# Two pairs of feed-forward chunks by seven half-depth products, the others with activations stationary, in a two-layer trunk on one core

## The chip, the cores and the metric

The kernel runs on one core of a Trainium2 chip. TensorE (PE in the views, its weight loads PEld) does the matmuls, VectorE (DVE) and ScalarE (ACT) the elementwise work, GpSimd (POOL) a few small operations, and SyncE (SP) issues the DMAs. The metric is the device time of one execution in microseconds, as the median over runs.

## What is computed

Two layers over x of 256 rows by 1024 columns, in float32. Each layer is a half-step SwiGLU feed-forward block, a mixer (a causal convolution module in layer 0, stick-breaking attention in layer 1) and a second feed-forward block; a root-mean-square norm stands ahead of each and at the end.

```python
D_MODEL, D_FF, SEQ, DEPTH = 1024, 2816, 256, 2
def swiglu_ffn(h, w_in, w_out):
    gate, up = jnp.split(h @ w_in, 2, axis=-1)
    return (jax.nn.silu(gate) * up) @ w_out
for i in range(DEPTH):
    g = norm_g[i]
    x = x + 0.5 * swiglu_ffn(rms_norm(x, g[0]), ffn_w_in[i, 0], ffn_w_out[i, 0])
    h = rms_norm(x, g[1])
    x = x + mixer(h)                 # conformer_conv in layer 0, attention in layer 1
    x = x + 0.5 * swiglu_ffn(rms_norm(x, g[2]), ffn_w_in[i, 1], ffn_w_out[i, 1])
return rms_norm(x, final_g)
```

There are thus four feed-forward blocks, here called FFN(0,0), FFN(0,1), FFN(1,0) and FFN(1,1), and they hold most of the matmuls.

## The kernel before

**Precision.** A float32 product is made of three matmuls: each operand is split into a rounded part `hi` and a rest `lo`, and `mm3` (L177) adds hi·hi, hi·lo and lo·hi. `split` (L147) makes the two parts: a ScalarE copy for hi, then a VectorE subtraction for lo. Weights arrive by DMA in float32 in a `raw` tile (pool `rawp`, 3 buffers) and are split into a `hi` and a `lo` tile (pool `ring`, 6 buffers of each).

**One feed-forward block.** The 256 rows are two tiles t = 0, 1 of 128. D_FF is cut into 11 chunks of 256 columns; a chunk j has 256 gate columns and 256 up columns, so 512 columns of `w_in`, 1024 deep, in two weight units of half the depth. `xT` holds the transposed, split input of both tiles, with the gain of the norm in it but not the row's factor `rstd`; that is applied behind the product. The chunks' outputs are multiplied with their rows of `w_out` by `V` (L309), 12 matmuls of 512 columns for each t, and add up in four PSUM banks `psv`. The V of a chunk stands one chunk later in the code, so that TensorE has work while VectorE and ScalarE make the gate.

A chunk has one of two forms. With activations stationary (`u_mm`, L227) each tile takes 24 matmuls of 512 columns into a PSUM tile `psu`; the gate (L267) makes a 128x256 tile, which TensorE turns by two transposes (`A`, L277) into V's stationary operand `ah`, `al`. With weights stationary (`C`, L287) the result comes out turned: `u_cm` (L235) runs four times in a chunk, for each half of the columns once for gate and once for up, with 8 matmuls of 512 columns (`psc`, L242 and L245) and 8 of 256 (L243). ScalarE and VectorE then add two halves (L247, L248), multiply by the row factors `rrow` (L294; on GpSimd in L298), and gate. Before the change chunk 0 (in FFN(0,0) chunks 0 and 1) has the first form and all others the second.

**Order.** Inside the feed-forward blocks a scheduler orders each engine's queue from the code and the tiles' dependencies. Each engine then works its queue in order: an instruction that waits holds up what stands behind it. In the convolution layer and at the very start of the kernel the order is written out by hand. The hand-written convolution casts the next block's first weight units in its course: `cast(nxt[0])` (L625) stands behind the taps of channel groups 6 and 7 for row tile 0 and ahead of those for row tile 1; the tap tables `wb` (L478) take buffers of the `ring` under the tags hi and lo too. `norm(0)` (L629) stands behind that cast on VectorE, and the turn of its result (`turn`, L556) is what TensorE does next after the last taps.

Of the kernel before, what the change touches and what calls it, by code (L numbers as in the profile page):

```python
# [8 lines left out]
F32 = mybir.dt.float32  # L9
F32R = mybir.dt.float32r  # L10
# [22 lines left out]
def trunk_kernel(  # L33
# [6 lines left out]
):  # L40
    nc = tc.nc
    first_pool = ctx.enter_context(tc.tile_pool(name="first_pool", bufs=1))
    ring = ctx.enter_context(tc.tile_pool(name="ring", bufs=6))
    operands = ctx.enter_context(tc.tile_pool(name="operands", bufs=1))
    rawp = ctx.enter_context(tc.tile_pool(name="rawp", bufs=3))
    acts = ctx.enter_context(tc.tile_pool(name="acts", bufs=1))
    const = ctx.enter_context(tc.tile_pool(name="const", bufs=1))
    wk = ctx.enter_context(tc.tile_pool(name="wk", bufs=2))
# [167 lines left out]
    def boundary(t, gi):  # L216

        for q in range(2):
            split_x(t, q, gain(turn_x(t, q), gi, q))
        return *operand(t), rms_stats(t)  # L220

    def u_step(ps, t, k, units):
        h, l = operand(t)
# [38 lines left out]

    def ffn(i, f, gi, hTs, next_gi, first=None, start=None, hook=None, final=False):
        w_in, w_out = ffn_w_in[i, f], ffn_w_out[i, f]
        act, aT = {}, {}

        def gate(t, j, ps):  # L267
            rstd = hTs[t][2]
# [18 lines left out]
        def C(j, units, rrow):  # L287

            hs, ls = [], []
            for q in range(2):  # L290
                for c in range(2):
                    u = u_cm([w[:, :, c, q * P : (q + 1) * P] for w in unit] for unit in units)
                    if c == 0:
                        nc.vector.tensor_tensor(u, u, rrow, op=ALU.mult)  # L294
# [3 lines left out]
                        nc.gpsimd.tensor_tensor(a, a, rrow, op=ALU.mult)  # L298
                    else:
                        nc.vector.tensor_tensor(a, a, u, op=ALU.mult)  # L300
                ah = operands.tile([P, T, P], F32R, tag="H", bufs=4, name=nm("ah"))
                al = operands.tile([P, T, P], F32R, tag="L", bufs=4, name=nm("al"))
                split(ah, al, a)
                hs.append(ah)
                ls.append(al)
            for t in range(T):
                aT[t, j] = [h[:, t, :] for h in hs], [l[:, t, :] for l in ls]

        def V(t, j, unit, qs=(0, 1)):  # L309
            ah, al = aT[t, j]  # L310
# [59 lines left out]
            for t in range(T)  # L370
        ]
        outs, vus = [None, None], []
        for j in range(NJ):
            if j == 0 and first:
                units = first
            elif not start or j >= lead:
                units = load_pairs(w_in, 256 * j, DFF + 256 * j, 256, pieces=2 if j else 4)
            if j == 0 or j >= lead:
                vus += [load_rows(w_out, 2 * c) for c in range(len(vus), j + 1)]
            if j == lead:  # L380
                rrow = row_rstd(hTs)
            if j < lead:
                if not start:
                    for t in range(T):
                        gate(t, j, u_mm(t, units))
                for t in range(T):
                    A(t, j)
            else:
                C(j, units, rrow)
            if j == NJ - 1:  # L390
                V(0, j - 1, vus[j - 1])
                V(1, j - 1, vus[j - 1], (0,))
                V(0, j, vus[j])
                finish = end_final if final else end
                outs[0] = finish(0)
                V(1, j - 1, vus[j - 1], (1,))
                V(1, j, vus[j])
                outs[1] = finish(1)
            elif j:
                for t in range(T):  # L400
                    V(t, j - 1, vus[j - 1])
            if j == 5 and hook:
                hook()
        return outs


# [397 lines left out]
    def start(gate):  # L804
# [31 lines left out]
        with tc.manual_schedule(engines={E.PE, E.SP, E.Activation, E.DVE}):  # L836
# [10 lines left out]
            xgs = [gain(pts[q], 0, q) for q in range(2)]  # L847
            for q in range(2):
                split_x(0, q, xgs[q])
            keep_busy(8)  # L850
            pts = [turn_x(1, q) for q in range(2)]
            cast(0, 0)
# [12 lines left out]
            mm(0, (1, 1), (1, 2), (0, 3))  # L865
            cast(0, 5)
            rstds.append(rms_stats(1))
            hTs.extend((*operand(t), rstds[t]) for t in range(T))
            mm(0, (1, 3), (0, 4))
            cast(0, 6)  # L870
            mm(0, (1, 4), (0, 5))
# [50 lines left out]
```

## Time and profile before

| | |
|---|---|
| median of 3 runs (lowest, highest) | 992.16 us (991.88 to 992.81) |
| the profiled execution: its time, its span | 992.41 us, 990.6 us |
| mean granted TensorE clock | 0.997 |
| busy share PE, PEld, DVE, ACT, POOL | 99%, 82%, 73%, 52%, 13% |
| HBM read | 171.10 MB |

The profiled execution's time is 1.8 us more than its span, which runs from the first to the last instruction. The share of an engine is its busy time over that span. Matmuls overlap in the records, so that of PE says only that something was always in flight.

### The profile page before, as it was taken

What the parts mean: (1) busy time and instruction counts of PE and PEld (TensorE: products, weight loads), DVE (VectorE), ACT (ScalarE), POOL (GpSimd) and SP (SyncE); (2) the same over time, 40 slices, a digit from 0 to 9 for tenths busy, and PEclk for the clock granted to TensorE, in tenths of its full rate; (3) what the DMA queues carried; (4) which work ended last, traced back from release to release, by engine and by line L of the source; (5) the groups of instructions that cost most, each with busy time, mean ns of one, the idle gap of its engine ahead of it and who ended that gap; (6) DMA issues with size and microseconds to landing.
All of it is one profiled execution on the core that took longest, in us unless ns stands there. A gap on an engine that the chain in (4) does not pass through costs nothing.

```text
span 990.6 us, 14730 instructions
## 1 busy us (share of the span) xinstructions
PE 977.4 (99%) x5658; PEld 813.6 (82%) x5658; DVE 722.3 (73%) x1127; ACT 514.0 (52%) x873; POOL 132.8 (13%) x165
## 2 busy tenths in 40 slices
PE   8999999999999999999999999999999999999996
PEld 7888888886788888888888888888777688888885
DVE  5886767659869776767876767676867887767654
ACT  6664545355437555455554545454644455554532
POOL 3011111100001111111211111112100011111111
PEclk9999999999999999999999999999999999999998
DMA  7976564447736564646456565654633344646411
GB/s 256 314 242 219 193 228 148 152 125 224 226 96 223 170 229 151 227 155 216 155 192 203 171 211 165 218 152 154 205 126 130 120 153 157 230 151 223 160 43 42
DMA packets 142630, 177.17 MB, mean 179 GB/s; under 512 B 6393, under 2 KB 125792, under 8 KB 142560
## 3 DMA queue, kind: packets, MB, share of 16 engines
q1 hardware_dynamic: 142208, 175.69, 54.5%
q8 instruction: 44, 0.72, 0.3%
q10 hardware_dynamic: 352, 0.55, 0.1%
q14 instruction: 26, 0.21, 0.1%
HBM read 171.10 MB, written 1.05 MB: 174 GB/s over the span
## 4 chain that ended last, share of the span: by engine, by line
PE 92%; DVE 3%; issue 2%; ACT 1%; DMA 1%; POOL 0%; SPq 0%; POOLq 0%; ACTq 0%; DVEq 0%
PE psc L242 28%; PE psc L243 16%; PE psv L178 8%; PE psv L180 8%; PE psv L179 8%; PE psc L245 4%; PE psu L178 3%; PE psu L179 3%; PE psu L180 3%; PE pc L506 3%; DVE lo L149 2%; PE ptr L200 1%; PE pz L700 1%; DMA raw<-in_ffn_w_in_dram 1%; ACT hi L148 1%
## 5 line engine op out<-in xcount | busy, mean ns | idle before, releaser
L149 DVE TENSOR_TENSOR lo<-raw,hi 128x1024 fp32r<-128x1024 f32 (+1 forms) x358 | 398.9, 1137 | 79.4 <-ACT hi L148 79.0
L242 PE MATMUL psc<-xT,hi 128*128 128x512 f32 x1204 | 433.4, 399 | 0.1
L148 ACT CAST hi<-raw 128x1024 fp32r<-128x1024 f32 (+1 forms) x360 | 327.5, 952 | 89.4 <-PE psc L242 34.1
L243 PE MATMUL psc<-xT,lo 128*128 128x256 f32 x1376 | 358.8, 281 | 0.0
L243 PEld LDWEIGHTS psc<-xT,lo 128*128 128x128 f32 x1376 | 260.0, 189 | 15.6 <-issue 0.4
L242 PEld LDWEIGHTS psc<-xT,hi 128*128 128x128 f32 x1204 | 226.6, 188 | 49.3 <-DVE u L248 0.4
L298 POOL TENSOR_TENSOR s<-s,rrow 128x256 f32<-128x256 f32 x78 | 90.7, 1163 | 580.1 <-DVE s L297 580.1
L178 PE MATMUL psv<-hi,ah 128*128 128x512 f32 x354 | 138.2, 390 | 0.3
L179 PE MATMUL psv<-lo,ah 128*128 128x512 f32 x354 | 137.6, 389 | 0.0
L180 PE MATMUL psv<-hi,al 128*128 128x512 f32 x354 | 137.1, 389 | 0.0
L247 ACT COPY u<-psc 128x256 f32<-128x256 f32 x172 | 63.5, 369 | 130.0 <-PE psc L245 129.9
L248 DVE TENSOR_TENSOR u<-psc,u 128x256 f32<-128x256 f32 x172 | 72.5, 421 | 78.4 <-ACT u L247 77.7
L148 ACT CAST ah<-s 128x256 fp32r<-128x256 f32 x78 | 31.7, 407 | 92.2 <-DVE s L300 92.0
L179 PEld LDWEIGHTS psv<-lo,ah 128*128 128x128 f32 x354 | 66.6, 188 | 13.8
L180 PEld LDWEIGHTS psv<-hi,al 128*128 128x128 f32 x354 | 66.4, 188 | 13.8
L178 PEld LDWEIGHTS psv<-hi,ah 128*128 128x128 f32 x354 | 66.5, 188 | 13.3 <-ACT ah L148 1.4
L178 PE MATMUL psu<-hi,xT 128*128 128x512 f32 x176 | 70.2, 399 | 0.2 <-ACT hi L148 0.2
L179 PE MATMUL psu<-lo,xT 128*128 128x512 f32 x176 | 69.3, 394 | 0.8 <-DVE lo L149 0.6
L180 PE MATMUL psu<-hi,xT 128*128 128x512 f32 x176 | 68.9, 391 | 0.0
L245 PE MATMUL psc<-xT,hi 128*128 128x512 f32 x172 | 68.4, 398 | 0.0
L296 ACT ACTIVATE s<-u 128x256 f32<-128x256 f32 x78 | 32.4, 415 | 47.7 <-DVE u L294 47.7
L149 DVE TENSOR_TENSOR al<-s,ah 128x256 fp32r<-128x256 f32 x78 | 33.0, 422 | 21.1 <-ACT ah L148 20.9
(134 smaller groups left out, 800.6 us busy)
## 6 DMA issues: line engine op xcount, KB each, us to landing
raw<-in_ffn_w_in_dram SPq DMA_DIRECT2D x168, 512.0 KB, 4.6
raw<-in_ffn_w_out_dram SPq DMA_DIRECT2D x44, 1024.0 KB, 4.8
raw<-in_conv_w_pw_dram SPq DMA_DIRECT2D x16, 512.0 KB, 4.6
raw<-in_attn_w_qkv_dram SPq DMA_DIRECT2D x16, 512.0 KB, 5.1
raw<-in_ffn_w_in_dram SPq DMA_DIRECT2D x16, 256.0 KB, 5.0
raw<-in_conv_w_pw_dram SPq DMA_DIRECT2D x4, 1024.0 KB, 4.9
raw<-in_attn_w_qkv_dram SPq DMA_DIRECT2D x4, 1024.0 KB, 5.0
raw<-in_attn_w_o_dram SPq DMA_DIRECT2D x4, 1024.0 KB, 4.7
```

The costliest lines, as they stand in the source:

```text
L148: copy(hi, src)
L149: (eng or nc.vector).tensor_tensor(lo, src, hi.bitcast(F32), op=ALU.subtract)
L178: nc.tensor.matmul(ps, lh, rh, start=start, stop=False)
L179: nc.tensor.matmul(ps, lh, rl, start=False, stop=False)
L180: nc.tensor.matmul(ps, ll, rh, start=False, stop=stop)
L242: nc.tensor.matmul(ps, h, xT[:, :, k, :, :], start=k == 0, stop=False)
L243: nc.tensor.matmul(ps[:, :, 0, :], l, xT[:, :, k, 0, :], start=False, stop=False)
L245: nc.tensor.matmul(ps, h, xT[:, :, k, :, :], start=False, stop=True)
L247: nc.scalar.copy(u, ps[:, :, 1, :])
L248: nc.vector.tensor_tensor(u, ps[:, :, 0, :], u, op=ALU.add)
L296: nc.scalar.activation(a, u, AF.Sigmoid)
L298: nc.gpsimd.tensor_tensor(a, a, rrow, op=ALU.mult)
```

## The change

Each block now follows a plan, `UUnUSUSUUUU`. U is a chunk with activations stationary. S is a pair of chunks by `strassen`. The letter n stands for `normalize`, which from then on puts the row factor into `xT` itself, so that the gate (`gate_normal`) has no factor any more. It also makes four sums and differences of quarters of the turned input (s1 to s4), each split again. The form C isn't used any more.

`strassen` takes the two row tiles and the two halves of the depth as a 2 by 2 matrix, the two halves of the depth and the two chunks as another, and multiplies them by seven products of half depth (12 matmuls of 512 columns each) where eight stood (Winograd's form). The weight differences are made in place in the raw tiles by `less`, the seven weight operands are split in 14 pieces of 128x1024, the sums of products are made by `plus` (seven of 128x512) with two copies out of PSUM by ScalarE (`keep`). `later` puts the V of the chunk ahead between the products. The pool `ring` goes from 6 buffers of each tag to 5, `rawp` from 3 to 5.

```diff
-    ring = ctx.enter_context(tc.tile_pool(name="ring", bufs=6))
+    ring = ctx.enter_context(tc.tile_pool(name="ring", bufs=5))
-    rawp = ctx.enter_context(tc.tile_pool(name="rawp", bufs=3))
+    rawp = ctx.enter_context(tc.tile_pool(name="rawp", bufs=5))
...
+        def gate_normal(t, j, src):
+            s = wk.tile([P, 256], F32, tag="A", bufs=13, name=nm("s"))
+            nc.scalar.activation(s, src[:, 0:256], AF.Sigmoid)
+            nc.vector.tensor_tensor(s, src[:, 0:256], s, op=ALU.mult)
+            nc.vector.tensor_tensor(s, src[:, 256:512], s, op=ALU.mult)
+            act[t, j] = s
...
+        def normalize():
+            x11, x12, x21, x22 = (xg for t in range(T) for xg in hTs[t][3])
+            for n, xg in enumerate((x11, x12, x21, x22)):
+                t, q = divmod(n, 2)
+                nc.vector.tensor_tensor(
+                    xg, xg, rrow[:, t, :].unsqueeze(1).broadcast_to([P, 4, P]), op=ALU.mult
+                )
+                split_x(t, q, xg)
+            normal.append(True)
+            def operand_of(dst, a, b, op):
+                nc.vector.tensor_tensor(dst, a, b, op=op)
+                hl = wk.tile([P, 2, 4, P], F32R, tag="sk", bufs=4, name=nm("sx"))
+                split(hl[:, 0], hl[:, 1], dst)
+                return hl[:, 0], hl[:, 1]
+            s1 = operand_of(x22, x21, x22, ALU.add)
+            s3 = operand_of(x21, x11, x21, ALU.subtract)
+            s2 = operand_of(x11, x22, x11, ALU.subtract)
+            s4 = operand_of(x12, x12, x11, ALU.subtract)
...
+        def strassen(ja, jb, later):
...
+            def cast(src):
+                hi, lo = (ring.tile([P, 4, 2, 256], F32R, tag=tag, name=nm(tag)) for tag in ("hi", "lo"))
+                for ks in pieces:
+                    split(hi[:, ks], lo[:, ks], src[:, ks])
+                return hi, lo
+            def less(dst, a, b):
+                for ks in pieces:
+                    nc.vector.tensor_tensor(dst[:, ks], a[:, ks], b[:, ks], op=ALU.subtract)
+            def product(ps, x, w):
+                for k in range(4):
+                    mm3(ps, x[0][:, k, :], x[1][:, k, :], w[0][:, k], w[1][:, k], k == 0, k == 3)
...
+            w = cast(b11)
+            product(px, old(0, 0), w)
+            less(b11, b12, b11)
+            w = cast(b11)
+            p1 = keep(px)
+            product(py, s1, w)
+            less(b11, b22, b11)
+            w = cast(b11)
+            p5 = keep(py)
+            product(px, s2, w)
+            w = cast(b21)
+            u2 = plus(px, p1)
+            product(py, old(0, 1), w)
+            later(0)
+            less(b12, b22, b12)
+            w = cast(b12)
+            gate_normal(0, ja, plus(py, p1, p1))
+            product(px, s3, w)
+            less(b21, b21, b11)
+            w = cast(b21)
+            u3 = plus(px, u2)
+            plus(u2, p5, u2)
+            product(py, old(1, 1), w)
+            gate_normal(1, jb, plus(u3, p5, p5))
+            w = cast(b22)
+            gate_normal(1, ja, plus(py, u3, u3))
+            product(px, s4, w)
+            gate_normal(0, jb, plus(px, u2, u2))
+            A(0, ja)
+            A(1, jb)
+            later(1)
+            A(1, ja)
+            A(0, jb)
...
+        plan = list("UUnUSUSUUUU" if start else "UUnUSUSUUUU")
...
+            if kind == "S":
+                before = waiting
+                def later(t):
+                    for c, tt in before:
+                        if tt == t:
+                            V(t, c, vus[c])
+                strassen(j, j + 1, later)
+                load_vus(j + 1)
+                waiting = [(j, 0), (j + 1, 1), (j, 1), (j + 1, 0)]
+                j += 2
...
+                if kind == "U":
+                    if j >= lead or not start:
+                        for t in range(T):
+                            gate(t, j, u_mm(t, units))
+                    for t in range(T):
+                        A(t, j)
...
+                else:
+                    finish_waiting()
+                    waiting = [(j, t) for t in range(T)]
```

The change moves instructions at three places that matter below. In the rows a name's trailing numbers are buffer numbers, and the brackets say on which engine or DMA queue an instruction waits.

**VectorE in the convolution layer.** `lo` is the rest of the next block's first weight unit (`cast(nxt[0])`), `pl` the turned tap results of row tile 0, x the residual, z the norm's result. Before:

```order
L622 TENSOR_TENSOR x_86<-x_86,b_2139 128x1024
L149 TENSOR_TENSOR lo_2731<-raw_2460,hi_2730 128x512 [waits DMAHW2_49,DMAHW1_49,Activation_49]
L149 TENSOR_TENSOR lo_2731<-raw_2460,hi_2730 128x512 [waits Activation_49] x3
L534 BN_STATS st_2613<-pl_2774 128x6 [waits PE_49]
L540 BN_AGGR mv_2814<-st_2613 128x2 [waits DVE_49]
L547 SCALAR_TENSOR_TENSOR z_2820<-pl_2614,mv_2814,fg 128x512 [waits DVE_49]
```

and now:

```order
L766 TENSOR_TENSOR x_86<-x_86,b_1965 128x1024
L149 TENSOR_TENSOR lo_2557<-raw_2286,hi_2556 128x512 [waits DMAHW1_49,DVE_49,DMAHW2_49,PE_49,Activation_49]
L149 TENSOR_TENSOR lo_2557<-raw_2286,hi_2556 128x512 [waits Activation_49] x3
L678 BN_STATS st_2439<-pl_2600 128x6
L684 BN_AGGR mv_2640<-st_2439 128x2 [waits DVE_49]
L691 SCALAR_TENSOR_TENSOR z_2646<-pl_2440,mv_2640,fg 128x512 [waits DVE_49]
```

The order is the same; with one buffer less the lo tile takes over the buffer of the tap table of channel groups 6 and 7, and so waits for TensorE, for the last matmul of `taps(7, 1)`; the statistics behind it no longer need a wait of their own. The hi tile takes over that of groups 4 and 5, and waits for `taps(5, 1)`.

**ScalarE where FFN(0,1) begins.** The first `hi` row is the second unit of its first chunk (`cast(nxt[1])`), the later ones weight units of the block; xg is the next block's input, quarter by quarter. Before:

```order
L148 CAST hi_3011<-raw_2557 128x512 [waits DMAHW4_49,DMAHW3_49]
L148 CAST hi_3011<-raw_2557 128x512 x3
L148 CAST xT<-xg_3052 128x4x128 [waits DVE_49,Activation_49]
L148 CAST hi_3129<-raw_3128 128x1024 [waits DMAHW5_49,PE_49]
L148 CAST hi_3129<-raw_3128 128x1024
L148 CAST xT<-xg_3061 128x4x128 [waits DVE_49,Activation_49]
```

and now:

```order
L148 CAST hi_2837<-raw_2383 128x512 [waits DMAHW4_49,DMAHW3_49,PE_49]
L148 CAST hi_2837<-raw_2383 128x512 x3
L148 CAST hi_2955<-raw_2954 128x1024 [waits DMAHW5_49,PE_49]
L148 CAST hi_2955<-raw_2954 128x1024
L148 CAST hi_3048<-raw_3047 128x1024 [waits DMAHW7_49,DMAHW6_49,PE_49]
L148 CAST xT<-xg_2878 128x4x128 [waits DVE_49,Activation_49]
L148 CAST hi_3048<-raw_3047 128x1024
L148 CAST hi_3057<-raw_3056 128x1024 [waits DMAHW1_49,DMAHW0_49,PE_49]
L148 CAST hi_3057<-raw_3056 128x1024
L148 CAST xT<-xg_2887 128x4x128 [waits DVE_49,Activation_49]
```

The first cast now waits for TensorE: its buffer comes free with the second k of the convolution's last output product, `out_mm(1, 1)`. Two more weight units have moved ahead of the quarters of the input.

**VectorE where a later block passes from its second chunk to the first S.** The rows are of FFN(0,1); the two other later blocks have the same order. Here `p`, `a` are the gate of the second chunk, `lo_3212` the second unit of the third chunk, `lo_3221` its `w_out` rows, `lo_3338` the split of b11. Before, a block's chunk of the form C looks like this:

```order
L149 TENSOR_TENSOR lo_7983<-raw_7981,hi_7982 128x1024 [waits Activation_49]
L248 TENSOR_TENSOR u_7931<-psc_7914,u_7931 128x256 [waits Activation_49]
L149 TENSOR_TENSOR lo_8115<-raw_8113,hi_8114 128x1024 [waits DMAHW7_49,DMAHW0_49,Activation_49]
L300 TENSOR_TENSOR s_7910<-s_7910,u_7931 128x256 [waits DVE_49,Pool_49]
L149 TENSOR_TENSOR lo_8115<-raw_8113,hi_8114 128x1024 [waits Activation_49]
L149 TENSOR_TENSOR al_7936<-s_7910,ah_7935 128x256 [waits Activation_49]
```

and now there stands, from the moment at which the second chunk's last matmul is done:

```order
L149 TENSOR_TENSOR xT<-xg_2930,xT 128x4x128 [waits PE_49,Activation_49]
L149 TENSOR_TENSOR lo_3212<-raw_3210,hi_3211 128x1024 [waits DMAHW7_49,DMAHW6_49,Activation_49]
L149 TENSOR_TENSOR lo_3212<-raw_3210,hi_3211 128x1024 [waits Activation_49]
L284 SCALAR_TENSOR_TENSOR p_3131<-psu_3104,rstd_441_2948,s_3129 128x256 [waits DMAHW3_49,Activation_49]
...
L335 TENSOR_TENSOR xg_2939<-xg_2930,xg_2939 128x512 [waits DVE_49]
L149 TENSOR_TENSOR lo_3221<-raw_3219,hi_3220 128x1024
L149 TENSOR_TENSOR sx_3186<-xg_2939,sx_3186 128x512 [waits Activation_49]
...
L273 TENSOR_TENSOR s_3252<-psu_3227,s_3252 128x256 [waits Activation_49]
L366 TENSOR_TENSOR raw_3323<-raw_3326,raw_3323 128x1024 [waits DMAHW4_49,DMAHW3_49]
L274 TENSOR_TENSOR s_3252<-psu_3227,s_3252 128x256 [waits DVE_49]
L366 TENSOR_TENSOR raw_3323<-raw_3326,raw_3323 128x1024
```

The new split of tile 1's input waits until the second chunk, which still reads the old one, has ended on TensorE; the four sums, the weights of the third chunk and the first weight differences all stand behind it in VectorE's queue.

## Rows read from the trace of the kernel before

**Rows 1.** the page: busy us (share of the span), instructions of each engine

```profile
PE 977.4 (99%) x5658; PEld 813.6 (82%) x5658; DVE 722.3 (73%) x1127; ACT 514.0 (52%) x873; POOL 132.8 (13%) x165
```

**Rows 2.** timeline of PE, chunk 1 of FFN(0,0): start, us, engine, line, operation

```profile
12.11 0.40 PE L179 MATMUL psu<-lo,xT 128*128 128x512 f32 x1
...
31.42 0.39 PE L180 MATMUL psu<-hi,xT 128*128 128x512 f32 x1
```

**Rows 3.** timeline of PE, two of the four u_cm of a chunk C

```profile
568.03 0.39 PE L242 MATMUL psc<-xT,hi 128*128 128x512 f32 x1
...
570.84 0.40 PE L242 MATMUL psc<-xT,hi 128*128 128x512 f32 x1
```

**Rows 4.** timeline of PE, from one turn of a gated tile to past the next

```profile
36.13 0.38 PE L281 MATMUL ptr<-ident,a 128*128 128x128 f32 x2
...
37.27 0.40 PE L179 MATMUL psv<-lo,ah 128*128 128x512 f32 x1
```

**Rows 5.** timeline of DVE, 128x1024 operations

```profile
246.94 4.63 DVE L149 TENSOR_TENSOR lo<-raw,hi 128x1024 fp32r<-128x1024 f32 x4
251.49 0.35 DVE L465 SCALAR_TENSOR_TENSOR up<-ptr,vec,sg 128x128 f32<-128x128 f32 x1
...
263.57 2.36 DVE L622 TENSOR_TENSOR x<-x,b 128x1024 f32<-128x1024 f32 x2
```

**Rows 6.** timeline of DVE, operations of 128x512 and of 128x256

```profile
302.56 0.68 DVE L206 TENSOR_TENSOR xg<-ptr,gvec 128x512 f32<-128x512 f32 x1
303.16 1.22 DVE L149 TENSOR_TENSOR lo<-raw,hi 128x1024 fp32r<-128x1024 f32 x1
...
316.12 0.42 DVE L149 TENSOR_TENSOR al<-ptr,ah 128x256 fp32r<-128x256 f32 x1
316.45 0.48 DVE L274 SCALAR_TENSOR_TENSOR a<-psu,rstd,p 128x256 f32<-128x256 f32 x1
...
560.37 0.42 DVE L248 TENSOR_TENSOR u<-psc,u 128x256 f32<-128x256 f32 x1 [0.91 <-ACT u L247]
560.83 0.43 DVE L294 TENSOR_TENSOR u<-u,rrow 128x256 f32<-128x256 f32 x1
```

**Rows 7.** timeline of PE, the last taps and the turn

```profile
271.77 2.15 PE L506 MATMUL pc<-sk,wb 128*32 128x128 f32 x67
274.56 1.94 PE L506 MATMUL pc<-sk,wb 128*32 128x128 f32 x61 [0.64 <-issue]
276.43 1.09 PE L560 MATMUL ptr<-ident,m 128*128 128x128 f32 x8
```

**Rows 8.** timeline of DVE, the cast of nxt[0] and norm(0)

```profile
267.90 2.50 DVE L149 TENSOR_TENSOR lo<-raw,hi 128x512 fp32r<-128x512 f32 x4 [1.98 <-ACT hi L148]
270.32 0.69 DVE L534 BATCH_NORM_STATS2 st<-pl 128x6 f32<-128x512 f32 x1
...
274.05 1.42 DVE L554 TENSOR_TENSOR m<-z,m 128x512 f32<-128x512 f32 x2
```

**Rows 9.** timeline of ACT, the casts of nxt[0] and nxt[1]

```profile
267.26 2.17 ACT L148 CAST hi<-raw 128x512 fp32r<-128x512 f32 x4
...
287.26 2.19 ACT L148 CAST hi<-raw 128x512 fp32r<-128x512 f32 x4
```

**Rows 10.** timeline of PE, out_mm(1, 1) and the start of FFN(0,1)

```profile
297.44 0.39 PE L180 MATMUL psv<-hi,xT 128*128 128x512 f32 x1
...
302.11 0.48 PE L178 MATMUL psu<-hi,xT 128*128 128x512 f32 x1
```

**Rows 11.** windows at the end: start:end, length, busy us (count) by engine, then granted clock

```profile
984.00:985.00 1.00, 0.00 (x0) 0.00 (x0) 0.56 (x3) 0.40 (x2) 0.00 (x0) 1.00 0.25 88
...
986.00:987.00 1.00, 0.00 (x0) 0.00 (x0) 0.75 (x1) 0.72 (x1) 0.00 (x0) 0.50 0.00 0
```

**Rows 12.** timeline of PE, turns of the input at the very start

```profile
4.09 1.86 PE L200 MATMUL ptr<-ident,x 128*128 128x128 f32 x8
...
6.66 1.04 PE L200 MATMUL ptr<-ident,x 128*128 128x128 f32 x8
```

More of the change, by code (lines that the diff above doesn't have):

```diff
@@ L216, in boundary @@
     def boundary(t, gi):
+        xgs = []
         for q in range(2):
-            split_x(t, q, gain(turn_x(t, q), gi, q))
-        return *operand(t), rms_stats(t)
+            xgs.append(gain(turn_x(t, q), gi, q))
+            split_x(t, q, xgs[q])
+        return *operand(t), rms_stats(t), xgs
     def u_step(ps, t, k, units):
@@ L264, in ffn @@
         w_in, w_out = ffn_w_in[i, f], ffn_w_out[i, f]
-        act, aT = {}, {}
+        act, aT, normal, sums = {}, {}, [], []
+        def gate_normal(t, j, src):
[4 more added lines that the diff above has]
+            act[t, j] = s
         def gate(t, j, ps):
+            if normal:
+                return gate_normal(t, j, ps)
             rstd = hTs[t][2]
@@ L297, in C @@
                         nc.vector.tensor_tensor(a, a, u, op=ALU.mult)
-                        nc.gpsimd.tensor_tensor(a, a, rrow, op=ALU.mult)
+                        if not normal:
+                            nc.gpsimd.tensor_tensor(a, a, rrow, op=ALU.mult)
                     else:
@@ new lines, in strassen, with old, plus, keep @@
+        def strassen(ja, jb, later):
+            wv = w_in.rearrange("(k p) n -> p k n", p=P)
+            raw = {}
+            for h, j in ((0, ja), (0, jb), (1, jb), (1, ja)):
+                raw[h, j] = rawp.tile([P, 4, 2, 256], F32, tag="raw", name=nm("raw"))
+                for c in range(2):
+                    c0 = c * DFF + 256 * j
+                    nc.sync.dma_start(raw[h, j][:, :, c, :], wv[:, 4 * h : 4 * h + 4, c0 : c0 + 256])
+            b11, b12, b21, b22 = raw[0, ja], raw[0, jb], raw[1, ja], raw[1, jb]
+            pieces = [slice(0, 2), slice(2, 4)]
+            def cast(src):
[9 more added lines that the diff above has]
+                    mm3(ps, x[0][:, k, :], x[1][:, k, :], w[0][:, k], w[1][:, k], k == 0, k == 3)
+            def old(t, q):
+                h, l = operand(t)
+                return h[:, 4 * q : 4 * q + 4, :], l[:, 4 * q : 4 * q + 4, :]
+            def plus(a, b, dst=None):
+                if dst is None:
+                    dst = wk.tile([P, 512], F32, tag="B", bufs=4, name=nm("sum"))
+                nc.vector.tensor_tensor(dst, a, b, op=ALU.add)
+                return dst
+            def keep(src):
+                dst = wk.tile([P, 512], F32, tag="B", bufs=4, name=nm("kept"))
+                nc.scalar.copy(dst, src)
+                return dst
+            s1, s2, s3, s4 = sums
+            px, py = (ps_u.tile([P, 512], F32, tag="u", name=nm("psp")) for _ in range(2))
+            w = cast(b11)
[31 more added lines that the diff above has]
+            A(0, jb)
@@ L372, in ffn @@
         outs, vus = [None, None], []
[L373 to L380, printed above, removed]
-                rrow = row_rstd(hTs)
-            if j < lead:
-                if not start:
-                    for t in range(T):
[L385 to L402, printed above, removed]
@@ L403, in ffn @@
                 hook()
+                hook = None
         return outs
@@ L846, in start @@
             pts = [turn_x(0, q) for q in range(2)]
-            xgs = [gain(pts[q], 0, q) for q in range(2)]
+            first_xgs = [gain(pts[q], 0, q) for q in range(2)]
             for q in range(2):
-                split_x(0, q, xgs[q])
+                split_x(0, q, first_xgs[q])
             keep_busy(8)
@@ L867, in start @@
             rstds.append(rms_stats(1))
-            hTs.extend((*operand(t), rstds[t]) for t in range(T))
+            hTs.extend((*operand(t), rstds[t], (first_xgs, xgs)[t]) for t in range(T))
             mm(0, (1, 3), (0, 4))
```

36 lines of the change are left out of this document (35 added, 1 removed).

## The prediction

> **What bounds the kernel now.** I read the page's busy shares first. TensorE is busy for 99% of the span, its weight loads for 82%, VectorE for 73% [rows 1]; with nearly no idle time left on TensorE, an edit gains what it takes off TensorE's queue, and loses each new wait of TensorE. Then I read TensorE's timeline for prices. A 512-column matmul takes 0.227 us in a row of its kind: 86 of them lie from the first to the last row of [rows 2], 19.31 us over 85 steps. One `u_cm` takes 2.81 us [rows 3], so a chunk C takes 4 x 2.81 = 11.25. Two transposes put between matmuls cost 0.23: in [rows 4], 1.14 us hold three matmuls of V (0.68) and two such pairs. VectorE next. Operations of 128x1024, two float32 inputs each, follow one another at 1.138 us (4.55 for four; the residual's addition, also float32, has the same length) [rows 5]. One of 128x512 takes 0.60; one of 128x256 takes 0.33 where it is independent of the one before, 0.46 where it needs its result [rows 6]. I take 0.61 and 0.40, with 0.33 and 0.46 as bounds.
>
> **What TensorE saves.** A chunk U takes 48 matmuls and two pairs of transposes, 48 x 0.227 + 0.46 = 11.34, 0.09 more than C (0.06 with 2.82 for `u_cm`, which other chunks show; I take 0.06). A pair S takes 7 x 12 = 84 matmuls and four pairs of transposes, 19.04 + 0.92 = 19.96, against 4 x 2 x 2.82 = 22.56 for two chunks C: -2.6. V doesn't change. FFN(0,0) trades five C for U and two pairs for S: -5.2 + 0.3 = -4.9. A later block trades six and two pairs: -4.84, three blocks -14.5. In all -19.4.
>
> **What VectorE gets.** A pair S adds eight `less` and seven `plus`, a block's `normalize` four products, four sums and eight splits. A chunk C had twelve operations of 128x256 beside its weights (5.1 us), a U has six (2.5). Summed by these prices VectorE goes from 722 us to some 840, 84% of the span and above the 82% of the weight loads. Judging engines by occupancy, the Trainium skill ("Perfetto Trace Analysis", Identifying the Most-Contended Engine) names the one with the highest as the one to improve, and counts for TensorE the weight loads, not the matmuls. By that rule VectorE becomes the bound on average; I count stage by stage, since its load isn't even.
>
> *First S of a later block.* The split of tile 1's normalised input waits until chunk 1's last matmul; from there VectorE's queue is full until the first lo piece of the next U. It holds 31 operations of 128x1024 (14 lo and 8 `less` of S, 2 for the second weight unit of chunk 2, 2 for its V, 4 for the V of the pair, the first of the next U), 15 of 128x512 behind that first split (the other split of tile 1, four sums, four splits of them, seven `plus`; 16 with the first), and 22 of 128x256. With 1.4 us until the first split ends (estimate: ScalarE's copy, as long as VectorE's 0.6, and the waits between engines), that is 1.4 + 31 x 1.138 + 16 x 0.61 + 22 x 0.40 = 55.2 (one 128x512 is counted too much, 0.6, for waits inside). TensorE has, up to the second matmul of that U, 222 matmuls (the V of chunk 0, chunk 2, the V of chunk 1, 84 of S, the V of chunk 2, and 30 more of V and U that the order puts ahead) and eight pairs of transposes: 222 x 0.227 + 1.8 = 52.2. TensorE waits 3.1 us (with 0.33 or 0.46: 1.6 to 4.4).
>
> *Second S of a later block.* From the end of the U between: VectorE 0.65 until the gate begins, 25 x 1.138 + 7 x 0.61 + 16 x 0.40 = 39.8; TensorE has 168 matmuls, since the V of two chunks lies in it, and six pairs: 39.5. Wait 0.3 (0 to 1.5). Together 3.4 for a block, **10.2** for three.
>
> *FFN(0,0).* There TensorE has less beside S. First S: 142 matmuls and six pairs, 33.6, against 0.6 + 24 x 1.138 + 4.3 + 6.4 = 38.6: 5.0. Second S: 158 matmuls and the small transposes of the convolution's constants, 37.7, against 39.8 and about 1 for copying those: 3.1, to which I add 0.5 because one copy waits for its transpose. The normalised input is some 1.2 late for chunk 2, since VectorE splits weights nearly without a gap there, and five raw buffers give back about 0.5. Sum 5.0 + 3.6 + 0.7 = 9.3 (6 to 12), net of the saving **+4.4**.
>
> **What the smaller ring does to the convolution.** The cast of the next block's first unit ran on ScalarE from 267.26 and on VectorE from 267.90 to 270.32; the statistics and `norm(0)` follow in VectorE's queue and end at 275.47 (274.05 + 1.42), and TensorE turned the result at 276.43, when its taps ended, waiting for nothing [rows 7 to 9]. Now the hi part waits for `taps(5, 1)` and the lo part for `taps(7, 1)`, which is TensorE's last work ahead of the turn. The hi casts, from about 271.3, hold two evictions of taps behind them on ScalarE, and since the taps of groups 6 and 7 need their PSUM buffers, `taps(7, 1)` ends near 277.7, not 276.5. Then come four lo pieces (2.4 us, [rows 8]), and from the first statistics to the end of the gating 5.15 us (270.32 to 275.47): 277.7 + 2.5 + 5.2 = 285.4. TensorE turns at 285.4 in place of 276.43, **+9.0** (8 to 10), of which it stands idle for 7.6. Nothing covers that: all TensorE work behind the turn needs its result.
>
> **TensorE's clock after that wait.** At the end of the kernel, with TensorE's last matmul started at 982.7, and nothing after it, the granted clock was 1.00 in the window from 984 and 0.50 in that from 986 [rows 11], 1.2 in place of 2.4 GHz. A wait of 7.6 us is longer than that idle stretch up to 986. What the return costs is shown by no row directly; the nearest is the very start, where eight transposes took 1.86 us from 4.09 and 1.04 from 6.66 [rows 12]; work at half pace lasted from 1.7 to about 5.8, so some 2 us were lost. I take **+2** (0 to 4). The Trainium skill ("TensorE: Matmul & The Clock Gate", Terms) puts such a loss at half of the time at the low clock; by it the 4.1 us at the start cost 2.05, the same.
>
> **Start of FFN(0,1).** Before, nxt[1] was cast from 287.26 [rows 9], long ahead. Now it waits for the second k of `out_mm(1, 1)`, whose last matmul began at 297.44 [rows 10]: 2.2 us from 297.7, then two pieces and one more of about 0.96 each (estimate from a half piece at 0.55 in [rows 9]), then xT: near 303.4 in place of 297, and the second quarter near 306.9. `psu` began at 302.11 [rows 10], and half its work, twelve matmuls, needs the second quarter (304.8 at the old pace). **+2.5** (0 to 4).
>
> **Nothing** for attention (order alone changes near its end; 1.5 either way) and for GpSimd, which loses L298. DMA reads the same bytes.
>
> **Sum.** Against the profiled execution's 992.41 (990.6 of span and 1.8 around it; 0.25 above the median): -14.5 + 10.2 + 4.4 + 9.0 + 2.0 + 2.5 = +13.6, so 1006.0, as a median **1005.8**.
>
> **Rivals.**
> *Each long wait costs the clock too.* The first S of each block and the second of FFN(0,0) make TensorE wait 3 to 5 us. If these waits lie in one piece, as the idle time at the end did, each costs up to 2 us again: 5 x 2 = 10, about 1016. For it: VectorE's queue feeds one product after another, and the wait falls at the end, at the next U. Against: the missing pieces come in one by one, with a product of 2.7 us between.
> *VectorE keeps ahead, and it is faster.* This takes the other side. If VectorE enters each S with its first differences and splits done, because it used gaps that my count leaves out, then the waits of 10.2 and 8.6 are gone, and the sum is -5.2: 987. It decides where that lead is more than 3 us in a later block and 5 in the first. Against it stands the order: the split of tile 1 waits for TensorE, and what could run ahead is queued behind it.
> *Half of that lead* gives 996, and with no cost for the clock and the start some 992, no difference. That the change does nothing can't be; the convolution's wait is certain from the order.
>
> **Chances.** Forecast, 998 to 1013: 0.58. Clock at each S, 1013 to 1024: 0.20. Above: 0.04. Between 994.1 and 998: 0.03. A measurement of this kernel can tell about 0.2% (2 us) from no change: within that 0.05, faster 0.10. So slower 0.85. The range must leave out no more than 0.2: from 992, with no cost for clock and start and half the waits, to 1020, the clock at most S stages. The forecast's own is 998 to 1013.
>
> **What would show it.** TensorE idle for 7 to 8 us in the convolution, ahead of the `ptr` of L556's turn, released by VectorE's m; the granted clock under 1 behind it. No chunk C; the U from 11.3 us. VectorE near 100% in each S and some 840 us in all; TensorE's waits there released by lo. `psu` of FFN(0,1) waiting for xT. I am wrong if VectorE shows gaps in S (prices or lead wrong), if the wait in S is far above 4 us a block, or if the turn comes before 283 on the new time line.

## The result: 0.9% slower, 1000.92 against 992.02 us

| | before | changed |
|---|---|---|
| median (lowest, highest) | 992.02 us (991.50 to 992.81), 4 runs | 1000.92 us (999.22 to 1002.69), 4 runs |
| ratio, 95% interval | | 1.0089 (1.0066 to 1.0113) |
| profiled execution: time, span | 992.41, 990.6 | 1002.69, 1000.6 |
| mean granted clock | 0.997 | 0.993 |

The change costs 8.9 us. The forecast was 1005.8, in a range from 992 to 1020, and slower with a chance of 0.85. The profiled execution lies 1.8 us above the median; the stages below are its own, +10.3.

First the page, busy shares and the engines of the chain that ended last:

```profile
PE 970.1 (97%) x5094; PEld 778.0 (78%) x5094; DVE 811.4 (81%) x1125; ACT 524.8 (52%) x813; POOL 41.8 (4%) x87
...
PE 84%; DVE 7%; ACT 4%; DMA 3%; issue 2%; SPq 1%; POOLq 0%; ACTq 0%; DVEq 0%
```

Against [rows 1], TensorE has 564 matmuls less and 97% in place of 99%: it now waits. VectorE has risen to 81%, past the weight loads' 78%. Then the waits of TensorE: what waited for what, us in total, times, the longest:

```profile
PE ptr L704 <- DVE m L698: 7.0, 1, 7.0
PE psv L178 <- ACT ah L148: 3.6, 4, 1.8
PE pc L650 <- ACT acc L656: 2.0, 1, 2.0
PE psv L179 <- DVE lo L149: 1.9, 4, 0.9
...
PE psu L180 <- DVE xT L149: 0.9, 1, 0.9
PE psp L179 <- DVE lo L149: 0.9, 1, 0.9
```

One wait of 7.0 us stands out, that of the turn in the convolution for VectorE's m. The waits for `ah` and, in `psv` and `psp`, for lo are all of FFN(0,0). To see what each stage gained or lost I take, in TensorE's timeline of both kernels, the start of the last turn of the input that ends each stage (the convolution ends at the first such turn, since in the changed kernel the second lies inside the next block):

| stage | before, us | changed, us | difference |
|---|---|---|---|
| to the end of FFN(0,0) | 197.83 | 205.80 | +8.0 |
| convolution | 97.59 | 107.98 | +10.4 |
| FFN(0,1) with its start | 194.60 | 193.43 | -1.2 |
| FFN(1,0) | 186.52 | 182.78 | -3.7 |
| attention | 123.14 | 122.69 | -0.5 |
| FFN(1,1) to the last matmul | 183.01 | 179.94 | -3.1 |

**The convolution.** TensorE's timeline of the changed kernel, the last taps and the two turns, as in [rows 7]:

```profile
282.38 3.70 PE L650 MATMUL pc<-sk,wb 128*32 128x128 f32 x128 [1.97 <-ACT acc L656]
293.10 1.97 PE L704 MATMUL ptr<-ident,m 128*128 128x128 f32 x8 [7.02 <-DVE m L698]
...
304.03 1.03 PE L704 MATMUL ptr<-ident,m 128*128 128x128 f32 x8
```

and VectorE's, the rows that answer to [rows 8]:

```profile
286.20 2.50 DVE L149 TENSOR_TENSOR lo<-raw,hi 128x512 fp32r<-128x512 f32 x4 [12.32 <-issue]
288.62 0.69 DVE L678 BATCH_NORM_STATS2 st<-pl 128x6 f32<-128x512 f32 x1
...
292.35 1.41 DVE L698 TENSOR_TENSOR m<-z,m 128x512 f32<-128x512 f32 x2
```

The four lo pieces began at 286.20, 0.12 us after the last taps (from 282.38, 3.70 us long), and the statistics, which no longer wait for anything of their own, began at 288.62 behind them. The view names no releaser for the 12.32 us that VectorE stood idle ahead of the pieces ("issue"); that it was TensorE follows from the time and from the wait in the program's order, and the experiments below test it. The turn started 7.02 us after TensorE had run out of work. Less what was already late, 8.0, it is 293.10 - 276.43 - 8.0 = 8.7 us later. The taps themselves show 1.97 us of waiting for ScalarE's eviction, which stood behind the hi casts.

The granted clock behind it (windows: start:end, length, busy us (count) of PE, PEld, DVE, ACT and POOL, then the clock, DMA share and rate in GB/s):

```profile
289.00:291.00 2.00, 0.00 (x0) 0.00 (x0) 1.93 (x5) 0.00 (x0) 0.74 (x2) 0.90 0.56 125
291.00:293.00 2.00, 0.00 (x0) 0.00 (x0) 1.97 (x3) 1.22 (x3) 0.00 (x0) 0.50 0.97 397
...
295.00:297.00 2.00, 2.00 (x9) 1.71 (x7) 1.84 (x3) 0.59 (x1) 0.00 (x0) 0.50 0.00 0
297.00:299.00 2.00, 2.00 (x9) 1.66 (x8) 1.93 (x5) 0.00 (x0) 0.74 (x2) 0.89 0.00 0
```

It fell to 0.50 in the idle time and rose in the window from 297. From the first turn to the second it was 304.03 - 293.10 = 10.9 us; before, [rows 7] to its second turn (285.67), 9.2. That is 1.7 for the clock.

**Start of FFN(0,1).** TensorE's first `psu` matmuls there, as in [rows 10]:

```profile
321.83 0.50 PE L178 MATMUL psu<-hi,xT 128*128 128x512 f32 x1 [0.48 <-ACT xT L148]
...
323.50 0.50 PE L180 MATMUL psu<-hi,xT 128*128 128x512 f32 x1 [0.94 <-DVE xT L149]
```

`psu` begins 8.05 us after the first turn of the input (313.78); before it was 6.69 (302.11 less 295.42). With the 0.94 behind it 2.3 us are lost here.

### The profile page after: what moved, and what is told of

Read it like the earlier page. It is cut to its first block, busy times and chain, and to the rows that moved or that the text cites. A ratio compares the mean times of both kernels' runs of the same rounds, so it can differ in the third digit from the quotient of the medians.

```text
span 1000.6 us, 13490 instructions
## 1 busy us (share of the span) xinstructions
PE 970.1 (97%) x5094; PEld 778.0 (78%) x5094; DVE 811.4 (81%) x1125; ACT 524.8 (52%) x813; POOL 41.8 (4%) x87
## 4 chain that ended last, share of the span: by engine, by line
PE 84%; DVE 7%; ACT 4%; DMA 3%; issue 2%; SPq 1%; POOLq 0%; ACTq 0%; DVEq 0%
PE psu L180 12%; PE psu L179 12%; PE psu L178 12%; PE psv L179 8%; PE psv L180 8%; PE psv L178 8%; PE psp L179 4%; PE psp L178 4%; PE psp L180 4%; DVE lo L149 3%; PE psc L244 3%; ACT hi L148 3%; PE pc L650 2%; PE ptr L293 2%; PE psc L245 2%
## 5 line engine op out<-in xcount | busy, mean ns | idle before, releaser
L149 DVE TENSOR_TENSOR lo<-raw,hi 128x1024 fp32r<-128x1024 f32 (+1 forms) x406 | 439.8, 1122 | 74.5 <-ACT hi L148 59.2
L148 ACT CAST hi<-raw 128x1024 fp32r<-128x1024 f32 (+1 forms) x408 | 372.8, 965 | 152.5 <-PE psu L180 52.2
L178 PE MATMUL psu<-hi,xT 128*128 128x512 f32 x544 | 213.3, 394 | 0.9 <-ACT xT L148 0.5
L180 PE MATMUL psu<-hi,xT 128*128 128x512 f32 x544 | 212.4, 390 | 0.9 <-DVE xT L149 0.9
L179 PE MATMUL psu<-lo,xT 128*128 128x512 f32 x544 | 212.4, 390 | 0.8 <-DVE lo L149 0.5
L178 PEld LDWEIGHTS psu<-hi,xT 128*128 128x128 f32 x544 | 102.2, 188 | 23.5 <-issue 1.2
L180 PEld LDWEIGHTS psu<-hi,xT 128*128 128x128 f32 x544 | 102.1, 188 | 22.7 <-DVE xT L149 1.7
L179 PEld LDWEIGHTS psu<-lo,xT 128*128 128x128 f32 x544 | 102.2, 188 | 22.6 <-DVE lo L149 1.1
L366 DVE TENSOR_TENSOR raw<-raw,raw 128x1024 f32<-128x1024 f32 x64 | 76.3, 1215 | 0.0
L179 PE MATMUL psp<-lo,sx 128*128 128x512 f32 x128 | 50.7, 396 | 0.1
L178 PE MATMUL psp<-hi,sx 128*128 128x512 f32 x128 | 50.3, 393 | 0.0
L180 PE MATMUL psp<-hi,sx 128*128 128x512 f32 x128 | 50.3, 393 | 0.0
L149 DVE TENSOR_TENSOR al<-ptr,ah 128x256 fp32r<-128x256 f32 x88 | 36.2, 416 | 6.4 <-ACT ah L148 6.3
```

The lines of the kernel that those rows point to most:

```text
L148: copy(hi, src)
L149: (eng or nc.vector).tensor_tensor(lo, src, hi.bitcast(F32), op=ALU.subtract)
L178: nc.tensor.matmul(ps, lh, rh, start=start, stop=False)
L179: nc.tensor.matmul(ps, lh, rl, start=False, stop=False)
L180: nc.tensor.matmul(ps, ll, rh, start=False, stop=stop)
L366: nc.vector.tensor_tensor(dst[:, ks], a[:, ks], b[:, ks], op=ALU.subtract)
```

## The experiments

Ratios are to the kernel before, run on the same chip.

**Only the pools changed.** The kernel before, with

```diff
-    ring = ctx.enter_context(tc.tile_pool(name="ring", bufs=6))
+    ring = ctx.enter_context(tc.tile_pool(name="ring", bufs=5))
-    rawp = ctx.enter_context(tc.tile_pool(name="rawp", bufs=3))
+    rawp = ctx.enter_context(tc.tile_pool(name="rawp", bufs=5))
```

> The kernel before with only the two pools changed (ring 5, rawp 5); all chunks as before. My theory: the pool change alone costs the convolution its wait and the block behind it a late start: 8.7 us later at the turn, 1.7 for the clock behind it and 2.3 at the start of FFN(0,1), together 12.7, so about 1004.7 us, a ratio near 1.013. The rival, that the loss comes from VectorE in the S stages and the pools cost nothing: 992, ratio 1.000.

Measured: 1005.61 us, ratio 1.0134 (1.0119 to 1.0150), so +13.3 by the ratio. The turn of the convolution in its trace:

```profile
283.60 2.11 PE L560 MATMUL ptr<-ident,m 128*128 128x128 f32 x8 [7.02 <-DVE m L554]
```

The same wait, with none of the new arithmetic in the kernel; the convolution takes 107.83 us and FFN(0,1) 196.70, 10.2 and 2.1 more than before, all other stages within 0.5. The pool change alone costs more than the whole change; the rest of it gains some 4 us. The two pools were not changed one by one; the order ahead of the prediction shows the turn's wait to hang on the buffers of `ring`.

**The first cast moved.** The changed kernel, with `cast(nxt[0])` behind both norms:

```diff
             taps(7, 0, 1, ps_u, "u")
-            cast(nxt[0])
             taps(4, 1, 1, ps_u, "u")
...
             out_mm(0, 1, turn_1)
+            cast(nxt[0])
             cast(nxt[1])
```

> The changed kernel with cast(nxt[0]) moved behind out_mm(0, 1), so that it stands behind norm(0) and norm(1) in VectorE's queue. My theory: the turn waits for its taps alone, the 7.0 us of idle TensorE and the 1.7 of low clock go, 10.4 us less than the changed kernel, about 990.5 (ratio to the kernel before 0.998); the late start of FFN(0,1) stays. The rival, that the wait is only displaced (the statistics are late for another reason, or the cast is late for FFN(0,1)): 996 to 1001.

Measured: 992.28 us, ratio 1.0002 (0.9986 to 1.0019): 8.6 us less than the change, where 10.4 were expected. In its profiled execution TensorE's turn no longer waits:

```profile
284.93 2.16 PE L650 MATMUL pc<-sk,wb 128*32 128x128 f32 x67 [2.05 <-issue]
287.02 1.09 PE L704 MATMUL ptr<-ident,m 128*128 128x128 f32 x8
...
296.24 1.03 PE L704 MATMUL ptr<-ident,m 128*128 128x128 f32 x8
```

The two turns lie 9.2 us apart, as before the change, so the clock's 1.7 is gone too. In this execution, which at 995.72 us lies 3.4 above the median, a wait of 2.05 us put down to "issue" stands ahead of the last taps (0.64 before, [rows 7]; 0.3 to 3.2 us in the other kernels whose trace has such a wait there); the convolution takes 99.50 us, 1.9 more than before. Whether that is what misses in the median isn't shown, and its cause I didn't settle. Three of the ten runs, at 989.1 to 989.5, are below the 990.5 that were expected.

**Both casts moved.** Further, `cast(nxt[1])` goes from ahead of `out_mm(1, 0)` to behind `boundary(0)`.

> The changed kernel with cast(nxt[0]) behind out_mm(0, 1) and cast(nxt[1]) behind boundary(0) in the written order, so that the quarters of FFN(0,1)'s input no longer stand behind it on ScalarE. My theory: of the time with the first cast alone moved, 992.3, the late psu (1.4 us by the trace of that run) and the wait for xT behind it (0.9) go, 2.3 together: 990.0, a ratio of 0.998. The rival, that the casts of the block's own weights that were queued ahead of the input do the harm: 992.

Measured: 991.24 us, ratio 1.0002 (0.9984 to 1.0020): no difference that can be told from the kernel above. The start did become early; no wait for xT is left in its trace. But from the first turn of the input to the end of FFN(0,1) it takes 193.33 us, against 193.41 with the first cast alone moved. TensorE has new waits in that block, at the end of the first S and in the second:

```profile
389.74 0.41 PE L293 MATMUL ptr<-ident,s 128*128 128x128 f32 x2 [0.90 <-DVE s L274]
...
438.14 0.73 PE L178 MATMUL psv<-hi,ah 128*128 128x512 f32 x2 [0.34 <-ACT ah L148]
```

There TensorE now waits 0.90 us for a gated tile, and in the second S 0.34 for another and 0.43 for lo, 1.7 in all. The first matmul of S did begin earlier, 52.8 us behind the first turn of the input against 55.4, and so did VectorE's four sums, by 2.8; by the end of the block that lead is gone. These are single executions: the same block took 192.32, 192.57 and 196.43 us in the three other traces below in which both casts are moved and its plan is the same, and 193.25, 193.43 and 194.22 in the three others with the late start. A gain of about 1 us isn't excluded, one of 2.3 isn't seen.

**No pairs.** The changed kernel with

```diff
-        plan = list("UUnUSUSUUUU" if start else "UUnUSUSUUUU")
+        plan = list("UUnUUUUUUUUU" if start else "UUnUUUUUUUUU")
```

> The changed kernel with the plan UUnUUUUUUUUU in every block, so no seven-product pairs; pools, normalize and all else stay. My theory: eight pairs save 20.9 us of TensorE's queue and give back, by the trace, some 10 in FFN(0,0) and 1 in each later block, so without them the time rises by about 8, to 1009 (ratio 1.017). The rival, that the S stages are bound by VectorE and gain nothing: 1001 or less (ratio 1.009 or less).

Measured: 1011.48 us, ratio 1.0192 (1.0177 to 1.0207), 10.6 more than the change. The stages tell more. The last turns of FFN(0,0), FFN(0,1) and FFN(1,0):

```profile
199.35 0.66 PE L200 MATMUL ptr<-ident,x 128*128 128x128 f32 x4
...
507.34 0.61 PE L200 MATMUL ptr<-ident,x 128*128 128x128 f32 x4
...
695.09 0.60 PE L200 MATMUL ptr<-ident,x 128*128 128x128 f32 x4
```

FFN(1,0) takes 695.09 - 507.34 = 187.75 without pairs and 182.78 with two: 5.0 gained of 5.4, the price of the 24 matmuls that two pairs save (24 x 0.227). FFN(0,1) gains 4.8 and FFN(1,1) 4.7. So in a later block the two pairs together lose only 0.5 to 0.7 us, where the forecast had 3.4 of waits; the waits listed for TensorE have none in S there. Other executions lose more: FFN(1,0) takes 182.8 to 184.2 us in the eight traces with this plan for it, and the changed kernel's is the shortest. In FFN(0,0) it is the other way round: 199.35 without pairs, 205.80 with them. There S loses 6.45 where it should gain 5.4, 11.9 us of waits and slow clock.

**The turn's wait filled.** The changed kernel with 50 transposes that nothing reads, between the last taps and the turn:

```diff
             taps(7, 1, 1, ps_u, "u")
+            spare = ps_t.tile([P, 4, P], F32, tag="tr", name="spare_t")
+            for _ in range(50):
+                nc.tensor.transpose(spare[:, 0, :], ident, ident)
             turn(0, 0)
```

> The changed kernel with 50 transposes of the identity into a spare PSUM tile on TensorE between the last taps and the turn, about 6.6 us of work that nothing reads, inside its wait of 7.0 us. My theory: the wait stays, the clock doesn't fall, and the 1.7 us that the two halves behind the turn took longer come back: about 999.2 (ratio 1.007). The rival, that those 1.7 us come from the pushed work and not from the clock: 1001 (ratio 1.009).

Measured: 1000.89 us, ratio 1.0085 (1.0072 to 1.0098): no difference. The trace shows that the clock's share did go, the two turns now lie 9.25 us apart as before the change:

```profile
292.23 0.66 PE L704 MATMUL ptr<-ident,m 128*128 128x128 f32 x4 [1.41 <-DVE m L698]
...
301.48 1.03 PE L704 MATMUL ptr<-ident,m 128*128 128x128 f32 x8
```

The 1.7 us at that place are thus the clock's; that the whole time falls by them is not shown, since 1.7 us are 0.17%, within the interval, and other waits in this execution were longer (0.94 and 0.91 us in the second S of two later blocks, which the changed kernel's trace doesn't have).

**No pairs in FFN(0,0).** Both casts moved, and `UUnUUUUUUUUU` for the first block alone.

> Both casts moved, and in FFN(0,0) alone no pair at all (UUnUUUUUUUUU). My theory: 6.4 us under the kernel with both casts moved, as the traces of the all-U kernel and the changed one show for that block: 983.6 (ratio 0.991). The rival, that the loss in FFN(0,0) is a matter of normalize and not of S: 990.

Measured: 985.68 us, ratio 0.9935 (0.9918 to 0.9951), 5.6 under the kernel with both casts moved (6.6 by the ratios; 6.4 were expected). It is S that loses in FFN(0,0), not `normalize`.

**The constants' loading moved.** The changed kernel with the hook behind chunk 9 (`if hook and j >= 9`).

> The changed kernel with the loading of the convolution's constants moved from behind the chunk 6 to behind chunk 9 of FFN(0,0), so past both pairs. If their DMAs and copies cause part of the waits of the pairs there: 2 to 4 us less, 997 to 999 (ratio 1.005 to 1.007). My theory, VectorE's missing lead and the raw buffers held by S: at most the 1 us of copies, so 1000 (ratio 1.008).

Measured: 1000.86 us, ratio 1.0097 (1.0081 to 1.0113): no difference in the whole time. In its trace FFN(0,0) does end earlier, at 201.92 us, against 205.60 to 207.11 in the four traces with the same plan and the hook at its old place, while the convolution takes 109.42, 1.4 more than in the change. In each of those four traces TensorE waits 1.4 to 2.0 us for an `ah` at the end of one of the two S; in this one it doesn't. Where the first cast alone is moved, that wait is in the second S (1.99 us at 143.76), long behind VectorE's last copy of the constants (110.89), so their loading is not needed for it; whether they make it more frequent one trace doesn't tell. They aren't the main cause: with the hook moved S still loses, 201.92 against 199.35 without pairs.

**The pairs of FFN(0,0) later.** A first plan, with both casts moved, put the second S directly ahead of the last chunk (`UUnUUUSUSUU`). The last chunk's branch forms the V of the one chunk before it alone, so this kernel leaves out the V of one of the 11 chunks of FFN(0,0), 24 matmuls or 5.4 us.

> Both casts moved, and in FFN(0,0) alone the plan UUnUUUSUSUU: the two pairs come three chunks later. My theory: S is slow in FFN(0,0) (6.4 us more than all U there, where it should save 5.2) because VectorE enters the first S without a lead, from start, normalize and splits that fill it without a gap; with three chunks U ahead it has a lead as in the later blocks, the 11.6 us shrink to some 1.5, and the time is 10 us under that with both casts moved, about 980 (ratio 0.988). The rival, that the constants' DMAs of the convolution or the missing V do it: 986 to 990.

Measured: 982.54 us, ratio 0.9911 (0.9896 to 0.9926). With the 5.4 us left out it settles nothing between the two. So once more, one chunk earlier and with all of V:

```diff
-        plan = list("UUnUSUSUUUU" if start else "UUnUSUSUUUU")
+        plan = list("UUnUUSUSUUU" if start else "UUnUSUSUUUU")
```

> Both casts moved, and in FFN(0,0) the plan UUnUUSUSUUU: the pairs one chunk later than in the change, with two chunks U behind them, all products kept. My theory, that S is slow in FFN(0,0) because VectorE enters it without a lead: the block gets about 7 us shorter than with both casts moved alone, 984 (ratio 0.992). The rival, that S in FFN(0,0) gains nothing wherever it stands: as without pairs there, 985.7 or more (ratio 0.994), or 991 if the position has no part in it.

Measured: 982.65 us, ratio 0.9908 (0.9891 to 0.9924): 8.6 us under the kernel with both casts moved (9.3 by the ratios), 7 were expected. The last turn of FFN(0,0):

```profile
194.88 0.66 PE L200 MATMUL ptr<-ident,x 128*128 128x128 f32 x4
```

It is at 194.88 in place of 205.80 in the change and 199.35 without pairs: in the new place S gains 4.5 of 5.4 there, with one more chunk U ahead of it. The plan also puts a chunk U between the constants' loading and the second pair.

**That plan in all blocks.**

> Both casts moved, and the plan UUnUUSUSUUU in all four blocks. My theory: the waits of 0.7 to 2.1 us at the turn of a gated tile at the end of the first S, which the traces with both casts moved show in the later blocks, come from the same missing lead, and go: 1 us less for each of three blocks than the kernel with the later plan in FFN(0,0) alone, some 981 (ratio 0.989). The rival, that VectorE is full in S whatever stands ahead: the same as that kernel, 984.

Measured: 981.18 us, ratio 0.9892 (0.9877 to 0.9906). Against the kernel above this is 1.5 us less with overlapping intervals, so not told apart. In the traces FFN(0,1) takes 181.91 us from the last turn of its input to the last turn of its result, in the kernel above 183.35, and the waits of 0.3 to 0.5 us in its second S are gone; FFN(1,0) differs by 0.5, FFN(1,1) by 0.6 the other way. This kernel beats the one before by 1.1%.

## Why the prediction was right, and where it wasn't

The sign and the main cause held. That the sum held too is in part luck, since two errors of opposite sign met in it: by the stage table the three later blocks with their start came out at -8.0 where -1.8 was forecast (-14.5 + 10.2 + 2.5), and FFN(0,0) at +8.0 where it was +4.4. The terms, by the profiled executions (+10.3 against a forecast of +13.6):

*Convolution, +9.0 forecast, 8.7 measured.* The wait, its place and its length (7.6 forecast, 7.02) were as the order of VectorE's queue let expect. Undoing it gives 8.6 us back by the medians, and the pools alone reproduce it.

*Clock, +2.0 forecast, 1.7 measured* between the two turns, and gone with the filled wait. The Trainium skill ("TensorE: Matmul & The Clock Gate", Terms) puts such a loss at half of the time at the low clock; by the windows above the work ran low from 293.1 to about 297.4 (0.89 in the last window), so 2.2 by that rule, an estimate, and the trace agrees to half a microsecond.

*Start of FFN(0,1), +2.5 forecast, 2.3 seen, no gain from removing it.* The wait is real, but taking it away gave nothing that the runs can tell: S follows, and TensorE waits there instead. As a term to be added to the sum it was wrong for this kernel; with chunks C behind it, in the kernel with only the pools changed, FFN(0,1) did take 2.1 us longer. The mechanism (the input behind three casts on ScalarE) was right; that it lies on the path that sets the end is not borne out.

*Waits in S in the later blocks, 10.2 forecast, 1.9 lost* (5.44 a block less 4.77, 4.97 and 4.70). The step that failed: "The split of tile 1's normalised input waits until chunk 1's last matmul". It comes in two quarters, each with its own wait. VectorE in FFN(1,0) of the changed kernel:

```profile
527.24 0.69 DVE L149 TENSOR_TENSOR xT<-xg,xT 128x512 fp32r<-128x512 f32 x1
528.19 2.36 DVE L149 TENSOR_TENSOR lo<-raw,hi 128x1024 fp32r<-128x1024 f32 x2 [0.26 <-ACT hi L148]
...
531.58 0.68 DVE L149 TENSOR_TENSOR xT<-xg,xT 128x512 fp32r<-128x512 f32 x1
...
545.94 1.21 DVE L366 TENSOR_TENSOR raw<-raw,raw 128x1024 f32<-128x1024 f32 x1
```

and TensorE, the first turn of the second chunk's gated tile, right behind that chunk's last matmul, and of the third chunk's:

```profile
529.29 0.38 PE L293 MATMUL ptr<-ident,a 128*128 128x128 f32 x2
...
546.15 0.38 PE L293 MATMUL ptr<-ident,s 128*128 128x128 f32 x2
```

The first quarter's split ran at 527.24, while the second half of chunk 1 was still on TensorE (to 529.29), and the weight splits behind it from 528.19. When the third chunk ended at 546.15, VectorE stood at the third `less` piece (545.94), about 2.5 us ahead of where the count had it: the count starts the weight splits 1.4 us behind 529.29, at 530.7, and they began at 528.19. The count was 3.1 us of wait for this S; the lead accounts for most of it. The durations were right: VectorE's queue runs nearly without a gap there, at the pitches of [rows 5] and [rows 6]. Its total was put too high, at some 840 us; the page has 811.4.

*FFN(0,0), +4.4 forecast, +8.0 measured.* The waits and the slow clock there cost 11.9 us by the kernel without pairs, where 9.3 were counted; another 1.0 is there without pairs too (199.35 against 197.83 before, where 0.5 was counted for the chunks U). A sign of being wrong that the prediction named, waits in S far above 4 us a block, is met in this block. The waits of the first S were taken as 5.0, and without the clock. At its end TensorE's timeline reads:

```profile
85.61 0.76 PE L178 MATMUL psv<-hi,ah 128*128 128x512 f32 x2 [0.59 <-ACT ah L148]
...
91.41 0.73 PE L178 MATMUL psv<-hi,ah 128*128 128x512 f32 x2 [1.76 <-ACT ah L148]
93.00 0.80 PE L179 MATMUL psv<-lo,ah 128*128 128x512 f32 x1 [0.86 <-DVE lo L149]
...
94.03 0.63 PE L179 MATMUL psv<-lo,ah 128*128 128x512 f32 x1
...
96.35 0.40 PE L179 MATMUL psv<-lo,ah 128*128 128x512 f32 x1
```

and ScalarE's, just ahead of the longest wait:

```profile
90.04 1.04 ACT L148 CAST hi<-raw 128x1024 fp32r<-128x1024 f32 x1 [1.19 <-DMA raw<-in_ffn_w_out_dram]
90.99 0.36 ACT L148 CAST ah<-ptr 128x256 fp32r<-128x256 f32 x1
```

TensorE waits for `ah` at 85.61 and 91.41 and for lo at 93.00, and then its matmuls start 0.42 us apart up to 95.7, against 0.23 from 96.35. The granted clock (windows as above) fell behind these waits:

```profile
90.00:92.00 2.00, 0.59 (x2) 0.30 (x2) 0.61 (x2) 1.96 (x3) 0.00 (x0) 1.00 0.28 81
92.00:94.00 2.00, 1.14 (x3) 0.83 (x3) 2.00 (x2) 0.31 (x1) 0.00 (x0) 0.66 0.08 12
94.00:96.00 2.00, 2.00 (x6) 1.59 (x5) 2.00 (x3) 0.00 (x0) 0.70 (x2) 0.50 0.62 181
```

So the rival "each long wait costs the clock too" came true at this one place, for about 1.5 us (each start-to-start distance less 0.227, summed from 93.0 to 96.35), and at no other S of the changed kernel. The longest wait went through ScalarE: a weight cast ahead of the gated tile waited 1.19 us for its DMA, which was issued at 82.28 and landed 7.7 us later (the page's median for this line is 4.8). By the code S works on four of the five raw buffers, which would make the issue late; the long landing has no cause shown. The forecast had no transfer in that sum. That VectorE's missing lead lets these transfers start late fits what the later place of S did; the experiment moves the lead, the transfers and the distance to the constants together, so which of them weighs more stays open.

*TensorE's saving, -19.4 forecast.* Seven products for eight are worth the matmul's price, less what the two items above lose. Chunks U cost a little more than forecast: without pairs FFN(1,0) takes 187.75 against 186.52 with chunks C, +1.2 where 0.6 were counted (ten chunks, 0.06 each).

The rival "VectorE keeps ahead" was right for the later blocks, with a lead of 2.5 us where it asked for 3, and wrong for FFN(0,0). The kernel is slower because of two stages, the convolution (+10.4) and FFN(0,0) (+8.0): undoing the first alone gives no difference from the kernel before (1.0002), and moving the second cast and placing the pairs of FFN(0,0) later as well gives 0.9908.

## What to carry to other kernels

A pool's size is part of every schedule that was written out by hand: with one buffer less, an early prefetch in an in-order queue becomes a barrier for what is queued behind it, and this cost more than the new arithmetic gained; moving two casts and starting the pairs a chunk later turned +0.9% into -1.1%. Where two engines are nearly balanced in a stage, count the lead with which the slower one enters, and for that each piece's own dependency, not the tile's; here 2.5 us of lead were most of a forecast wait of 3.1. A wait that is shown on the engine is worth removing only when no later stage takes it over.

## What the runs showed that I had not expected

The clock fell in FFN(0,0) behind waits of 0.59, 1.76 and 0.86 us with matmuls between them, not only behind a wait as long as the convolution's: matmul starts went from 0.23 to 0.42 us apart. In the kernel without pairs in FFN(0,0) a lone wait at the end of the first S of FFN(0,1) did the same:

```profile
379.49 0.41 PE L293 MATMUL ptr<-ident,s 128*128 128x128 f32 x2 [2.09 <-DVE s L274]
```

The granted clock is 1.00 in the window from 378 and 0.50 in those from 380 to 383, and that block took 196.43 us. So the rival of the clock at S does come true in some executions, in a later block too. It doesn't always: the wait of 2.05 us in the taps where the first cast alone is moved has a clock of 1.00 behind it.

The last taps of the convolution wait for "issue" by 0.4 to 3.2 us in the kernels whose turn doesn't wait for VectorE, with no cause shown. Without the turn's wait, the changed kernel's ten timed runs spread from 989.1 to 995.8 us, where those of the kernel before spread from 990.4 to 993.8 on the same chip (and from 990.4 to 995.4 on another).
